# Moving transposes, projections and channel-major steps later in the slots of an attention loop

## The chip, the cores and the metric

The kernel runs on one core of one Trainium2 chip. The metric is the device time of one execution in microseconds; the median of three runs of the kernel before is 972.73 us (972.63 to 973.1). Five engines work in parallel, each through its own instructions in a fixed order: TensorE (PE; its weight loads are listed as PEld), VectorE (DVE), ScalarE (ACT), GpSimd (POOL) and SyncE (SP), which issues the DMA transfers.

## The reference

Four residual layers over 512 frames of 1024 channels: a pooling mixer, a gated MLP with a causal convolution, chunked attention with 16 heads of 64 channels, and a second gated MLP. The change touches the attention alone. What it computes:

```python
h = rmsnorm(x, mix_norm[i])
qkv = h @ w_qkv
q = head_rmsnorm(q, q_norm)          # per head, over its 64 channels
k = head_rmsnorm(k, k_norm)
s = einsum('bqhd,bkhd->bhqk', qc, kb) * scale + bias   # band of 9 chunks of 64 keys
p = softmax(where(valid, s, -1e30))
o = einsum('bhqk,bkhd->bqhd', p, vb)
x = x + o @ w_o
```

All values are float32. The kernel makes its products from a high and a low part of each factor, with three matmuls for one product in the projections.

## The kernel before

The attention is the middle of the program. Queries and keys are projected in four groups, `project(0)` to `project(3)`; group c holds heads 4c to 4c + 3, so it feeds head pairs 2c and 2c + 1. Each projection accumulates four tiles in PSUM over 96 matmuls (L123 to L125, tiles `qk`). The tiles are then copied out as `Z[c, t]` (L964 on DVE, L966 on ACT), squared (L956), reduced (L957) and normalised: a chain of small steps (L974, L975, L135 and L136 on ACT, L137 to L139, L977) makes one factor per frame and head, and L979 multiplies the four `Z` tiles by it on POOL.

Per head pair two channel-major steps (`channel_major`, four transposes each at L1032, tiles `zt`) turn the normalised queries and then the keys. Four DMA moves on SP (L1046) put halves where the second head of the pair needs them.

The 16 heads make 64 tiles of 128 queries, one tile a slot of the loop. In its slot i a tile goes through these steps, in this order on PE:

- `scores` of tile i: two matmuls (L1062, L1063), then on DVE the bias and row minimum (L1066), on ACT the exponential and its sum (L1068), on DVE a reciprocal (L1069), on ACT the scaling (L1070, tile `sb`);
- a channel-major step of the next pair, where i modulo 8 is in `CM`;
- `turn` of tile i - LAG: one to four transposes (L1078, tiles `tp`), which ACT and DVE split into high and low parts (L102, L103, tiles `pt`);
- after the last tile of a head, LAGM slots later, `mix`: eight matmuls with the values (L1090, tiles `oo`), copied by ACT (L1095) and added by DVE into the pair's output (L1096).

All PSUM tiles of these steps, `sc`, `zt`, `tp` and `oo`, share four banks (tag "S"). Each `sb` tile of a place in a head has one buffer.

Between the steps PE runs matmuls of a filler: `project(1)` up to slot FE[0], `project(2)` up to FE[1], `project(3)` up to FE[2], and from there the output projection of the first six pairs (L123 to L125, tiles `wo`, added to `X` at L1016) up to slot 64 + FO. `fill(upto)` issues as many of its matmuls as are due at that point of a slot. A pair's output is split into high and low parts (L102, L103, tiles `two`) before the output projection reads it.

PE's order in the loop is thus written by hand with the numbers LAG, LAGM, FE, FO and CM. The orders of DVE, ACT, POOL and SP are made by the framework's scheduler at build time.

Of the kernel before, what the change touches and what calls it, by code (L numbers as in the profile page):

```python
# [43 lines left out]
BANKS = {"PQ": 2, "SS": 4}  # L44


LAG, LAGM = 2, 2
FE = (3.5, 19.5, 35.5)
FO = LAG + 6
CM = (2, 3)  # L50


KIND = "uuppp" + "s" * 17
# [19 lines left out]
def trunk(ctx: ExitStack, tc: tile.TileContext, xt, xT, cols, band, edge, poolw, gv, wout, wqk, wv, wo, rel, out):  # L73
# [23 lines left out]
    def split(raw, hi, lo, eng=None, eng_hi=None):  # L97

        if eng_hi:
            eng_hi.tensor_copy(hi, raw)  # L100
        else:
            nc.scalar.activation(hi, raw, AF.Copy)  # L102
        return (eng or nc.vector).tensor_sub(lo, raw, hi.bitcast(F32))  # L103
# [23 lines left out]
    def run(steps):  # L127
        step = None
        for step in steps:
            pass  # L130
        return step
# [785 lines left out]
    def attention():  # L917
# [104 lines left out]
        def outputs():  # L1022
            yield from output(range(4))
            yield from output((4, 5))

        def channel_major(p, i):


            zt = psum("S", f"zt{p}_{i}", 4)
            for t in range(TT):  # L1030
                j = 4 * i + 2 * (p % 2)
                nc.tensor.transpose(zt[:, t * P:(t + 1) * P], Z[p // 2, t][:, j:j + 2, :].rearrange("p h d -> p (h d)"), ident)  # L1032
            zh, z2 = (big.tile([P, S], F32R, name=f"z{c}{p}_{i}", tag="zqk", bufs=8) for c in "h2")
            zl = None if i else g_tile(f"zl{p}_{i}")
            if i:
                nc.scalar.activation(zh, zt, AF.Copy, scale=gq[:, i:i + 1])
                for e in range(2):
                    hs = slice(e * HD, (e + 1) * HD)
                    nc.vector.scalar_tensor_tensor(KL[p % 2][e][hs], zt[hs], gq[hs, i:i + 1], zh[hs].bitcast(F32), op0=OP.mult, op1=OP.subtract)
            else:  # L1040
                split_scaled(zt, gq[:, i:i + 1], zh, zl)

            nc.gpsimd.tensor_copy(z2[HD:], zh[HD:].bitcast(F32))
            moves = [(z2[:HD], (z2 if i else zl)[HD:]), (zh[HD:], (zh if i else zl)[:HD])]
            for o, x in moves:
                nc.sync.dma_start(o.bitcast(F32), x if x.dtype == F32 else x.bitcast(F32))  # L1046
            QK[p, i] = (zh, z2)

        def scores(h, t):

            p, e = divmod(h, 2)
            q, k, kl = QK[p, 0][e], QK[p, 1][e], KL[p % 2][e]
            if t == 0:

                base = rdram[h, :]
                for r, n in ((0, S - HD), (HD, S)):
                    nc.sync.dma_start(BT[h % 2][r:r + HD, S - n:], bass.AP(tensor=base.tensor, offset=base.offset + HD, ap=[[1, HD], [1, n]]))
            n = (t + 1) * P
            nw = max(n, 256)

            sc = psum("S", f"sc{h}_{t}", 4)
            nc.tensor.matmul(sc[:, :nw], q[:, t * P:n], k[:, :nw], start=True, stop=False)  # L1062
            nc.tensor.matmul(sc[:, :nw], q[:, t * P:n], kl[:, :nw], start=False, stop=True)  # L1063
            SM[h, t] = s_ = big.tile([P, n], F32, name=f"sb{h}_{t}", tag=f"sb{t}")
            mx = tmp.tile([P, 3], F32, name=f"mx{h}_{t}", tag="mx", bufs=4)
            nc.vector.tensor_tensor_reduce(out=s_[:, :n], in0=sc[:, :n], in1=BT[h % 2][:, :n][:, ::-1], scale=1.0,  # L1066
                                           scalar=3e38, op0=OP.add, op1=OP.min, accum_out=mx[:, 0:1])
            nc.scalar.activation(s_[:, :n], s_[:, :n], AF.Exp, scale=-1.0, bias=mx[:, 0:1], accum_out=mx[:, 1:2])  # L1068
            nc.vector.reciprocal(mx[:, 2:3], mx[:, 1:2])  # L1069
            nc.scalar.activation(s_[:, :n], s_[:, :n], AF.Copy, scale=mx[:, 2:3])  # L1070

        def turn(h, t):

            n = (t + 1) * P
            s_ = SM.pop((h, t))
            tp = psum("S", f"tp{h}_{t}", 4)
            for j in range(t + 1):
                nc.tensor.transpose(tp[:, j * P:(j + 1) * P], s_[:, j * P:(j + 1) * P], ident)  # L1078
            split(tp[:, :n].rearrange("p (j q) -> p j q", q=P), *(x[:, t:4 * t + 1:3] for x in PT[h % 2]))

        def mix(h):

            p, e = divmod(h, 2)
            hs = slice(e * HD, (e + 1) * HD)
            oo = psum("S", f"oo{h}", 4)
            if p not in O2:
                O2[p] = big.tile([P, S], F32, name=f"o2_{p}", tag="o2", bufs=4)
            for c in range(2):
                for j in range(TT):
                    nc.tensor.matmul(oo[:, j * P:], V[j, h // 4][:, h % 4].rearrange("p a d -> p (a d)"),  # L1090
                                     PT[e][c][:, 4 * j:3 * j + TT].rearrange("p t q -> p (t q)"),
                                     start=j == 0 and c == 0, stop=j == TT - 1 and c == 1)
            ob = g_tile(f"ob{h}")
            other = slice(HD - e * HD, 2 * HD - e * HD)
            nc.scalar.activation(ob[hs], oo[other], AF.Copy)  # L1095
            nc.vector.tensor_add(O2[p][hs], oo[hs], ob[hs])  # L1096
# [13 lines left out]
        nb = len(tiles_)  # L1110
        fillers = [(project(1), 96, -3, FE[0]), (project(2), 96, FE[0], FE[1]), (project(3), 96, FE[1], FE[2]), (outputs(), 144, FE[2], nb + FO)]

        with tc.manual_schedule(engines={mybir.EngineType.PE}):
            cur, done, kept = 0, 0, 0

            def fill(upto):

                nonlocal cur, done
                while cur < len(fillers):
                    g, n, a, b = fillers[cur]  # L1120
                    due = n * (upto - a) / (b - a)
                    while done < min(due, n):
                        next(g)
                        done += 1
                    if upto < b:
                        return
                    run(g)
                    cur, done = cur + 1, 0

            fill(0)  # L1130
            for i in range(nb + LAG + LAGM):
                steps = []
                if i < nb:
                    steps.append(lambda: scores(*tiles_[i]))
                if i % 8 in CM and i // 8 + 1 < NPAIR:
                    steps.append(lambda: channel_major(i // 8 + 1, CM.index(i % 8)))
                j = i - LAG
                if 0 <= j < nb:
                    steps.append(lambda: turn(*tiles_[j]))
                j2 = j - LAGM  # L1140
                if 0 <= j2 < nb and j2 % TT == TT - 1:
                    steps.append(lambda: mix(tiles_[j2][0]))
                for x, step in enumerate(steps):
                    step()
                    if late and x < 2:
                        late.pop(0)()
                    fill(i + (x + 1) / len(steps))

                while 8 * kept + 7 <= j2 and (cur == 3 or cur == 2 and done >= 24 * (kept // 2 + 1)):
                    split(O2[kept], XS[kept], XS[KD + kept])  # L1150
                    kept += 1
            fill(nb + FO)
# [37 lines left out]
    with tc.tile_pool(name="ba", bufs=1) as big:  # L1190
        rest = attention()
# [55 lines left out]
```

## Time and profile before

| | before |
|---|---|
| median of three runs | 972.73 us |
| profiled execution, its own time | 972.73 us |
| its span, first to last instruction | 970.9 us |
| PE busy in the span | 962.8 us |
| attention loop, 456.4 to 606.2 us | 149.8 us |
| PE busy in it | 147.86 us |
| ACT busy in it | 131.23 us |
| DVE busy in it | 115.44 us |
| POOL busy in it | 62.46 us |

A row of the timeline gives start and length in us, engine, line, operation, written tile <- read tiles, shape and how many such instructions it merges; in brackets the idle time of the engine ahead of it and what ended it. A row of waits gives engine, line and tile, what it waited for, the sum in us, how often, and the longest. A row of the chain of waits gives start, length, engine and line. A row of DMA issues ends with the median us from issue to landing. Records of matmuls overlap, so a busy PE is not necessarily at its peak.

### The profile page before, as it was taken

What the parts mean: (1) busy time and instruction counts of PE and PEld (TensorE: products, weight loads), DVE (VectorE), ACT (ScalarE), POOL (GpSimd) and SP (SyncE); (2) the same over time, 40 slices, a digit from 0 to 9 for tenths busy, and PEclk for the clock granted to TensorE, in tenths of its full rate; (3) what the DMA queues carried; (4) which work ended last, traced back from release to release, by engine and by line L of the source; (5) the groups of instructions that cost most, each with busy time, mean ns of one, the idle gap of its engine ahead of it and who ended that gap; (6) DMA issues with size and microseconds to landing.
All of it is one profiled execution on the core that took longest, in us unless ns stands there. A gap on an engine that the chain in (4) does not pass through costs nothing.

```text
span 970.9 us, 13813 instructions
## 1 busy us (share of the span) xinstructions
PE 962.8 (99%) x5038; PEld 819.1 (84%) x5038; DVE 804.9 (83%) x1452; ACT 575.4 (59%) x990; POOL 103.1 (11%) x90
## 2 busy tenths in 40 slices
PE   9999999999999999999999999999999999999998
PEld 8788988888888888888888787888998888888886
DVE  8999989999899855442777888999989999989953
ACT  7665554655555544345898988646555565566531
POOL 2300000000000013204534532000000000000000
PEclk9999999999999999999999999999999999999999
DMA  8222332332323234332343341332323233332323
GB/s 342 73 96 71 114 107 81 120 119 88 108 77 119 78 84 147 92 121 92 111 115 106 97 118 55 101 108 80 116 91 102 89 120 106 107 101 79 114 81 110
DMA packets 37428, 102.83 MB, mean 106 GB/s; under 512 B 4432, under 2 KB 7904, under 8 KB 37360
## 3 DMA queue, kind: packets, MB, share of 16 engines
q1 hardware_dynamic: 37296, 101.90, 32.4%
q8 instruction: 40, 0.66, 0.3%
q14 instruction: 28, 0.23, 0.1%
q0 software_dynamic: 32, 0.04, 0.0%
q10 hardware_dynamic: 32, 0.00, 0.0%
HBM read 95.60 MB, written 2.14 MB: 101 GB/s over the span
## 4 chain that ended last, share of the span: by engine, by line
PE 94%; DVE 4%; ACT 2%; issue 0%; DMA 0%; DVEq 0%; ACTq 0%
PE st_m L610 11%; PE out L124 8%; PE out L125 8%; PE out L123 8%; PE st_m L612 5%; PE st_t L610 5%; PE gv L124 4%; PE gv L125 4%; PE gv L123 4%; PE qk L124 3%; PE qk L123 3%; PE qk L125 3%; PE st_t L612 3%; PE st_b L610 3%; PE tp L1078 2%; PE oo L1090 2%
## 5 line engine op out<-in xcount | busy, mean ns | idle before, releaser
L124 PE MATMUL out<-one,ow_h 128*128 128x512 f32 x224 | 88.0, 393 | 0.0
L123 PE MATMUL out<-one,ow_h 128*128 128x512 f32 x224 | 87.8, 392 | 0.0
L125 PE MATMUL out<-one,ow_l 128*128 128x512 f32 x224 | 87.8, 392 | 0.0
L833 DVE TENSOR_TENSOR X<-out,X 128x512 f32<-128x512 f32 (+1 forms) x65 | 44.3, 682 | 50.2 <-PE out L125 49.9
L409 ACT ACTIVATE ow_h<-wo_r 128x640 fp32r<-128x640 f32 (+1 forms) x64 | 50.4, 787 | 55.0 <-PE out L124 46.5
L610 PE MATMUL st_m<-two,g_h 128*128 128x512 f32 x224 | 70.0, 394 | 0.0
L610 PE MATMUL st_m<-h,g_h 128*128 128x512 f32 x224 | 69.1, 389 | 0.0
L410 DVE TENSOR_TENSOR ow_l<-wo_r,ow_h 128x640 fp32r<-128x640 f32 (+1 forms) x64 | 56.8, 888 | 2.5 <-ACT ow_h L409 2.5
L424 DVE SCALAR_TENSOR_TENSOR c<-a,col,c 128x511 f32<-128x511 f32 (+1 forms) x76 | 56.6, 747 | 0.0
L125 PE MATMUL qk<-wqk_h,two 128*128 128x512 f32 x128 | 51.4, 402 | 0.0
L123 PE MATMUL qk<-wqk_h,two 128*128 128x512 f32 x128 | 50.8, 409 | 0.0
L124 PE MATMUL qk<-wqk_l,two 128*128 128x512 f32 x128 | 50.8, 397 | 0.0
L610 PEld LDWEIGHTS st_m<-h,g_h 128*128 128x128 f32 x224 | 42.1, 188 | 9.6
L619 ACT ACTIVATE w<-st_m 128x512 f32<-128x512 f32 x28 | 16.7, 598 | 56.0 <-PE st_m L612 56.0
L612 PEld LDWEIGHTS st_m<-two,g_l 128*128 128x128 f32 x224 | 42.0, 188 | 8.8
L610 PEld LDWEIGHTS st_m<-two,g_h 128*128 128x128 f32 x224 | 41.1, 188 | 9.3 <-ACT w L619 0.8
L124 PEld LDWEIGHTS out<-one,ow_h 128*128 128x128 f32 x224 | 42.3, 189 | 6.3 <-DVE one L435 0.3
L125 PEld LDWEIGHTS out<-one,ow_l 128*128 128x128 f32 x224 | 42.3, 189 | 6.3
L123 PEld LDWEIGHTS out<-one,ow_h 128*128 128x128 f32 x224 | 42.3, 189 | 6.0
L1066 DVE CUSTOM_DVE_ANT_0 sb<-sc,B 128x128 f32<-128x128 f32 (+1 forms) x64 | 31.1, 486 | 18.9 <-PE sc L1063 18.0
L612 PE MATMUL st_m<-h,g_l 128*128 128x256 f32 x224 | 45.1, 283 | 0.0
L421 ACT ACTIVATE c<-a,col 128x512 f32<-128x512 f32 x38 | 30.7, 813 | 23.8 <-DVE a L768 22.0
(378 smaller groups left out, 2999.5 us busy)
## 6 DMA issues: line engine op xcount, KB each, us to landing
gv_r<-gv SPq DMA_DIRECT2D x86, 512.0 KB, 3.8
wo_r<-wout SPq DMA_DIRECT2D x32, 384.0 KB, 3.1
wo_r<-wout SPq DMA_DIRECT2D x32, 320.0 KB, 2.9
wqk_r<-wqk SPq DMA_DIRECT2D x16, 512.0 KB, 3.4
wv_r<-wv SPq DMA_DIRECT2D x8, 512.0 KB, 3.5
wo_r<-wo SPq DMA_DIRECT2D x8, 512.0 KB, 3.4
xt<-xt SPq DMA_DIRECT2D x4, 512.0 KB, 5.3
X<-xT SPq DMA_DIRECT2D x8, 256.0 KB, 7.3
```

The costliest lines, as they stand in the source:

```text
L123: yield nc.tensor.matmul(o, sh, mh, start=first, stop=False, **how)
L124: yield nc.tensor.matmul(o, sh, ml, start=False, stop=False, **how)
L125: yield nc.tensor.matmul(o, sl, mh, start=False, stop=last, **how)
L409: nc.scalar.activation(hi[:, :n], raw[:, :n], AF.Copy)
L410: return hi, lo, lambda: nc.vector.tensor_sub(lo[:, :n], raw[:, :n], hi[:, :n].bitcast(F32))
L421: nc.scalar.activation(c, a, AF.Identity, scale=cw[2], bias=cw[3])
L424: nc.vector.scalar_tensor_tensor(c[:, j:], a[:, :S - j], cw[2 - j], c[:, j:], op0=OP.mult, op1=OP.add)
L610: nc.tensor.matmul(o, hi[:, c], B[i, name], start=first and i == 0, stop=False, **how)
L612: nc.tensor.matmul(o[:, 0], lo[:, c], B[i, name][:, 0], start=False, stop=i == 3, **how)
L833: nc.vector.tensor_add(X[d][:, fs], o[:, fs], X[d][:, fs])
L1066: nc.vector.tensor_tensor_reduce(out=s_[:, :n], in0=sc[:, :n], in1=BT[h % 2][:, :n][:, ::-1], scale=1.0, scalar=3e38, op0=OP.add, op1=OP.m ...
L1078: nc.tensor.transpose(tp[:, j * P:(j + 1) * P], s_[:, j * P:(j + 1) * P], ident)
```

## The change

```diff
-LAG, LAGM = 2, 2
-FE = (3.5, 19.5, 35.5)
+LAG, LAGM = 3, 2
+FE = (5.5, 21.5, 37.5)
 FO = LAG + 6
-CM = (2, 3)
+CM = (3, 4)
...
                     fill(i + (x + 1) / len(steps))
+                fill(i + 1)
```

A tile's transposes now come three slots behind its scores, and with them the mix of a head, five slots behind its last scores instead of four. The three later projections end at slots 5.5, 21.5 and 37.5, and the channel-major steps stand in slots 3 and 4 of each eight. FO follows LAG, so the spread of the output projection ends at slot 73 instead of 72. The new `fill(i + 1)` acts only in a slot without steps, of which there is one near the end.

The same instructions are issued on every engine; their order changes. Three places follow. In the names, a number behind `sc`, `sb`, `mx` or `tp` is the head and the tile (`sc10_2`: head 10, third tile), behind `zt` the pair and query or key step, behind `qk` or `z` the projection, behind `o2` the pair, and the last number is only a buffer's.

DVE, the last steps of the normalisation of `project(3)`, which feeds pairs 6 and 7. Before:

```order
L137 SCALAR_TENSOR_TENSOR qk3_t_4894<-qk3_y_4893 128x32
L1066 ISA sb9_3_5496,mx9_3_5497<-sc9_3_5493,B1_3660 128x512
L1066 ISA mx9_3_5497 128x1
L1069 RECIPROCAL mx9_2_5478<-mx9_2_5478 128x1
L138 TENSOR_TENSOR qk3_t_4894<-qk3_t_4894,qk3_a_4892 128x32
L139 SCALAR_TENSOR_TENSOR qk3_y_4893<-qk3_t_4894,qk3_y_4893 128x32
L977 TENSOR_TENSOR qk3_y_4893<-qk3_y_4893,n1_y_3806 128x32
```

Now:

```order
L1096 TENSOR_TENSOR o2_4_5518<-oo8_5517,ob8_5527 64x512
L137 SCALAR_TENSOR_TENSOR qk3_t_4935<-qk3_y_4934 128x32
L138 TENSOR_TENSOR qk3_t_4935<-qk3_t_4935,qk3_a_4933 128x32
L1066 ISA sb10_2_5554,mx10_2_5555<-sc10_2_5551,B0_3659 128x384
L1066 ISA mx10_2_5555 128x1
L139 SCALAR_TENSOR_TENSOR qk3_y_4934<-qk3_t_4935,qk3_y_4934 128x32
L1069 RECIPROCAL mx10_1_5536<-mx10_1_5536 128x1
L977 TENSOR_TENSOR qk3_y_4934<-qk3_y_4934,n1_y_3806 128x32
```

L977, the last step ahead of POOL's L979, stood behind the L1066 of head 9, tile 3, and stands behind that of head 10, tile 2.

PE, from the scores of head 10, tile 2 to the first channel-major step of pair 6. Now:

```order
L1063 MATMUL sc10_2_5551<-kl10_3653,zh5_0_5341 128x384
L124 MATMUL wo1_0_5515<-two5_101,wo0_0_h_5439 128x512
L125 MATMUL wo1_0_5515<-two1_97,wo0_0_l_5440 128x512
L1078 MATMUL tp9_3_5562<-ident_106,sb9_3_5483 128x128 x4
L123 MATMUL wo1_0_5515<-two1_97,wo0_0_h_5439 128x512
L124 MATMUL wo1_0_5515<-two5_101,wo0_0_h_5439 128x512
L1062 MATMUL sc10_3_5571<-zh5_1_5379,zh5_0_5341 128x512
L1063 MATMUL sc10_3_5571<-kl10_3653,zh5_0_5341 128x512
L125 MATMUL wo1_0_5515<-two1_97,wo0_0_l_5440 128x512
L1032 MATMUL zt6_0_5581<-ident_106,z3_0_5316 128x128
```

Before, the channel-major step stood ahead of the scores of head 10, tile 3, one slot earlier; the transposes of head 9, tile 3 stood ahead of the scores of tile 2 and come after them now.

DVE, the same steps of the normalisation of `project(2)`, which feeds pairs 4 and 5. Before:

```order
L138 TENSOR_TENSOR qk2_t_4399<-qk2_t_4399,qk2_a_4397 128x32
L1069 RECIPROCAL mx5_2_4980<-mx5_2_4980 128x1
L139 SCALAR_TENSOR_TENSOR qk2_y_4398<-qk2_t_4399,qk2_y_4398 128x32
L1066 ISA sb5_3_4998,mx5_3_4999<-sc5_3_4995,B1_3660 128x512
L1066 ISA mx5_3_4999 128x1
L103 TENSOR_TENSOR pt1l_3650<-tp5_0_4988,pt1h_3649 128x128
L977 TENSOR_TENSOR qk2_y_4398<-qk2_y_4398,n1_y_3806 128x32
L103 TENSOR_TENSOR two4_100<-o2_1_4749,two0_96 128x512
```

Now:

```order
L1066 ISA sb6_1_5036,mx6_1_5037<-sc6_1_5033,B0_3659 128x256
L1066 ISA mx6_1_5037 128x1
L138 TENSOR_TENSOR qk2_t_4430<-qk2_t_4430,qk2_a_4428 128x32
L139 SCALAR_TENSOR_TENSOR qk2_y_4429<-qk2_t_4430,qk2_y_4429 128x32
L1096 TENSOR_TENSOR o2_2_5020<-oo4_5019,ob4_5029 64x512
L977 TENSOR_TENSOR qk2_y_4429<-qk2_y_4429,n1_y_3806 128x32
L103 TENSOR_TENSOR two4_100<-o2_1_4748,two0_96 128x512
```

L977 moved behind L1066 of head 6, tile 1 and behind L1096, the addition of the mix of head 4; the split of pair 1's output (`two4`) still follows it.

## The prediction

> **What bounds the kernel now.** I read the page's busy times first, then busy time in windows over the attention loop, the waits there, and the timeline at the places that stood out.
>
> ```profile
> span 970.9 us, 13813 instructions
> PE 962.8 (99%) x5038; PEld 819.1 (84%) x5038; DVE 804.9 (83%) x1452; ACT 575.4 (59%) x990; POOL 103.1 (11%) x90
> ```
>
> TensorE (PE) sets the end. Its instructions are the same in both kernels, in another order, so only its waits can move the time. The changed numbers act in the attention loop, 456 to 606 us. Columns: window, length, busy time of PE, weight loads, VectorE (DVE), ScalarE (ACT), GpSimd (POOL), granted clock, DMA.
>
> ```profile
> 540.00:560.00 20.00, 19.09 (x108) 15.23 (x107) 17.23 (x55) 18.05 (x48) 9.84 (x10) 1.00 0.27 78
> ...
> 600.00:610.00 10.00, 9.19 (x48) 7.40 (x47) 7.79 (x15) 6.36 (x12) 0.00 (x0) 1.00 0.17 54
> ```
>
> PE is idle 0.91 us in the first and 0.81 in the last of these windows. That undercounts, as the next rows show: a matmul is recorded for 0.39 us, but the next starts 0.23 us after it, so 0.16 us of each wait lies under a record. I price waits by starts.
>
> ```profile
> 589.57 0.39 PE L125 MATMUL wo<-two,wo_l 128*128 128x512 f32 x1
> 589.80 0.40 PE L123 MATMUL wo<-two,wo_h 128*128 128x512 f32 x1
> 590.37 0.33 PE L1078 MATMUL tp<-ident,sb 128*128 128x128 f32 x1 [0.18 <-ACT sb L1070]
> ...
> 599.96 0.75 PE L1090 MATMUL oo<-pt0h,one 128*128 128x512 f32 x4
> 600.55 0.80 PE L1090 MATMUL oo<-pt0l,one 128*128 128x512 f32 x4
> 601.18 0.44 PE L124 MATMUL wo<-two,wo_h 128*128 128x512 f32 x1
> 601.91 0.55 PE L1078 MATMUL tp<-ident,sb 128*128 128x128 f32 x3 [0.28 <-ACT sb L1070]
> ...
> 604.58 0.78 PE L1090 MATMUL oo<-pt1h,one 128*128 128x512 f32 x4
> 605.88 0.50 PE L1090 MATMUL oo<-pt1l,one 128*128 128x512 f32 x1 [0.53 <-DVE pt1l L103]
> ```
>
> Transposes (L1078) wait for ACT's scaled scores (L1070), and the last mix (L1090) for DVE's low parts (L103): 0.57 - 0.23 = 0.34, 0.73 - 0.23 = 0.50 and 1.30 - 0.59 = 0.71 us (0.59 is the same step unhindered, 599.96 to 600.55). Two more:
>
> ```profile
> 549.85 0.50 PE L124 MATMUL wo<-two,wo_h 128*128 128x512 f32 x1 [0.67 <-DVE two L103]
> ...
> 551.68 0.40 PE L123 MATMUL wo<-two,wo_h 128*128 128x512 f32 x1
> 552.17 0.44 PE L1078 MATMUL tp<-ident,sb 128*128 128x128 f32 x2
> ```
>
> The output projection waits for the split of a finished head pair, 0.67 shown and 0.16 hidden, 0.8 us, and a transpose 0.49 - 0.23 = 0.26. Last, a place that waits for nothing yet, the channel-major transposes of pair 6 (L1032), which read what POOL normalises at L979:
>
> ```profile
> 552.80 0.19 DVE L139 SCALAR_TENSOR_TENSOR qk_y<-qk_t,qk_y 128x32 f32<-128x32 f32 x1
> 553.03 0.19 DVE L977 TENSOR_TENSOR qk_y<-qk_y,n_y 128x32 f32<-128x32 f32 x1
> 553.30 4.05 POOL L979 TENSOR_TENSOR z<-z,qk_y 128x512 f32<-128x512 f32 x4 [5.82 <-DVE qk_y L977]
> 557.49 0.34 PE L1063 MATMUL sc<-kl,zh 128*128 128x384 f32 x1
> 557.86 0.56 DVE L1066 CUSTOM_DVE_ANT_0 sb<-sc,B 128x384 f32<-128x384 f32 x1
> 557.89 0.60 PE L1032 MATMUL zt<-ident,z 128*128 128x128 f32 x4
> 558.34 0.08 DVE L1066 DVE_READ_ACCUMULATOR2_ANT mx<- 128x1 f32 x1
> ```
>
> POOL ends at 557.35 and PE starts at 557.89: 0.54 us to spare. For pair 4 the same spare is 520.70 - 518.59 = 2.11 us:
>
> ```profile
> 514.09 4.50 POOL L979 TENSOR_TENSOR z<-z,qk_y 128x512 f32<-128x512 f32 x4 [5.55 <-DVE qk_y L977]
> 520.70 0.44 PE zt L1032 x4
> ```
>
> **The change part by part.** FE puts the end of each later projection two slots later, CM the channel-major step that reads its result one slot later. From the one to the other stay 11 - 5.5 = 5.5 slots of 10 - 3.5 = 6.5. A slot is (557.89 - 520.70) / 16 = 2.3 us, from the first channel-major step of pair 4 to that of pair 6, so every spare shrinks by about that. Pair 6 has none left.
>
> *Pair 6.* The order makes it sharper. DVE's L977 now stands behind the softmax step L1066 of head 10, tile 2, and that waits for PE's scores sc10_2; before, it stood behind head 9, tile 3, three score steps earlier. Count from T, the start of the second sc10_2 matmul (L1063). L1066 starts at T + 0.37 (557.49 to 557.86), the next instruction 0.48 later, L977 another 0.23 (552.80 to 553.03), POOL 0.27 after that, and its four products take 4.05: T + 5.40. On PE follow 0.18 for the scores, two matmuls, four transposes, two matmuls, the two 512-wide scores and a matmul. From these rows and the first fence on PE:
>
> ```profile
> 588.31 0.60 PE L1078 MATMUL tp<-ident,sb 128*128 128x128 f32 x4
> 588.66 0.48 PE L123 MATMUL wo<-two,wo_h 128*128 128x512 f32 x1
> 588.98 0.40 PE L124 MATMUL wo<-two,wo_h 128*128 128x512 f32 x1
> 589.39 0.34 PE L1063 MATMUL sc<-kl,zh 128*128 128x384 f32 x1
> ```
>
> four transposes cost 0.35 and 0.09 more on the matmul behind them (588.66 to 588.98 is 0.32, not 0.23), so 0.18 + 0.46 + 0.44 + 0.46 + 0.46 + 0.23 = 2.23, and the fourth channel-major transpose is due 0.3 later, at T + 2.5. PE waits 5.4 - 2.5 = **2.9 us**. Bounds 2.4 (all handovers at 0.1) and 3.3 (POOL at 4.50). Both sides hang on the same T, so earlier waits cancel.
>
> *Pairs 2 and 4.* L977 now stands behind the head addition L1096, which waits for the mix. T is the start of the second sc6_1 matmul; the mix's second half starts 0.63 (600.55 to 601.18) and two short steps before it, about 1.0.
>
> ```profile
> 593.16 0.80 PE L1090 MATMUL oo<-pt1l,one 128*128 128x512 f32 x4
> ...
> 594.94 0.69 DVE L1096 TENSOR_TENSOR o<-oo,ob 64x512 f32<-64x512 f32 x1
> ```
>
> L1096 comes 1.78 after that half, so at T + 0.8; DVE reaches it at about T + 1.05, after L1066 (0.37, and under 0.48 for its two parts), L138 and L139. L977 is 0.6 later, POOL 0.27 later: T + 5.95 with products of 4.05, T + 6.4 with 4.50. PE gets to the fourth transpose after 14 matmuls (3.22), seven transposes (0.61, and 0.18 behind them), the rest of three score steps (0.12, half a 512-wide matmul, then 0.36 and 0.46) and 0.3: T + 5.25. So 0.7 us for pair 2 and, where DVE's next row is the same split of a head pair as at 514.13, 1.15 for pair 4: **1.85**, bounds 0 and 2.4.
>
> ```profile
> 514.13 1.55 DVE L103 TENSOR_TENSOR two<-o,two 128x512 fp32r<-128x512 f32 x1
> ```
>
> That split took 1.55 us there beside POOL's 4.50. [...]
>
> *The later transposes* take away the waits for scaled scores and, with two more fills ahead of it, the last mix's: 0.34 + 0.50 + 0.26 + 0.71 = **-1.8 us** (bounds -2.2 with smaller ones, -1.2 if one stays).
>
> *The split's wait* of 0.8: the split of pair 3 is put out at the end of slot 36 for the tenth output matmul, due at 37.5 + 9 / 4.06 = 39.7; before, at the end of slot 35 for 35.5 + 9 / 3.95 = 37.8. So it has 2.7 slots instead of 1.8, but waits behind the same queue on ACT and DVE. I take half, **-0.4** (0 to -1.1).
>
> *Closer spacing in the channel-major slots.* PE now goes from one step to the next past 256-wide scores instead of 512-wide ones (two matmuls of 0.23), and DVE has the longest L1066 just ahead. The banks of the score ring come free up to 0.35 us later against PE, in six such pairs: 0 to 2.1; today only pairs 6 and 7 show such waits, so I take a quarter, **+0.5**. The rest (fills per slot 96 / 8.5 = 11.3 instead of 96 / 6.5 = 14.8 at first, and 144 / 35.5 = 4.06 for 144 / 36.5 = 3.95 at the end) moves no work off PE.
>
> Sum: 2.9 + 1.85 - 1.8 - 0.4 + 0.5 = +3.05. The profiled execution took 972.73 us, its span of 970.9 and 1.83 around it, and is itself the median of the three runs: 972.73 + 3.05 = **975.8 us**.
>
> **Rivals.**
> 1. *More is taken away than starts show (the other side).* The waits of PE's weight loads (PEld) count in full, since the loads end last in these steps.
>
> ```profile
> PEld tp L1078 <- ACT sb L1070: 3.1, 8, 0.6
> PEld wo L124 <- DVE two L103: 1.0, 1, 1.0
> PEld oo L1090 <- DVE pt1l L103: 0.7, 1, 0.7
> ```
>
> Then 4.8 go instead of 2.2: 2.9 + 1.85 + 0.5 - 4.8 = +0.45, 973.2 us, not slower by what can be told. It decides from 3.3 of these 4.8 on. Against it: loads run ahead of matmuls, and where starts can be compared they lost 0.26 to 0.50 on a transpose, with 0.6 the longest wait of a load. Chance 0.07.
> 2. *Pairs 2 and 4 keep their cover.* The spare of 2.11 nearly outlasts the slot; only pair 6 waits, and no bank does: 972.73 + 2.9 - 1.8 - 0.4 = 973.4. For it: spare and slot are within 0.2. Against it: L1096 ahead of L977. Chance 0.19.
> 3. *Pair 6's halves land late.* They are moved by DMA before the scores of pair 6 read them.
>
> ```profile
> 563.65 0.54 SPq L1046 DMA_DIRECT2D zh<-zh  x1
> zh<-zh SPq DMA_DIRECT2D x8, 128.0 KB, 2.3
> 574.13 0.44 PE zt L1032 x4
> ```
>
> The first transposes at 557.89 led to the last move at 563.65 and a landing 2.3 later, 8.1 us. From there to the first score five slots stay of six, each (574.13 - 557.89) / 8 = 2.0 now: 10.1, less the part of the slot ahead of the transposes. If over 1 us of the remainder goes, pairs 6 and 7 add 1 each: 977.8. Chance 0.08.
>
> 4. *The gap slows the clock.* Every window above has a granted clock of 1.00, with gaps up to 0.8 us. If a gap of 2.9 let it fall to half for as long, it would cost 1.4 more: 977.2. [...] Chance 0.03.
>
> **How the numbers follow.** The forecast has 0.63, with a range of its own of 974.5 to 977.2. 8 in 10 with the rivals: 973.4 (rival 2) to 977.8 (rival 3). A measurement here tells 0.2% (1.95 us) from no change. Slower by more, above 974.7: 0.63 + 0.08 + 0.03, less 0.02 for the forecast's low end, 0.72. Faster, under 970.8: only rivals 1 and 2 together get there (2.9 - 4.8 = -1.9), 0.03. Within: the rest, 0.25.
>
> **What would show it.** Right: PE's transposes L1032 of pair 6 wait for POOL's L979 in three steps of about 0.8, 2.5 to 3.3 us together; those of pairs 2 and 4 by 0.4 to 1.3 each; no wait of L1078 for L1070 and none at the last mix. Wrong: pair 6's transposes start with no wait, or L977 runs before sc10_2; a wait of scores (L1062) for a DMA (rival 3); a clock under 1.00 after 560 us (rival 4).

## The result, and the profile after

The changed kernel takes 977.51 us (median of four executions: 976.59, 977.45, 977.57, 977.98), the kernel before 972.71 beside it: a ratio of 1.0047, 95% interval 1.0035 to 1.0060. It is slower by 4.8 us. The forecast was 975.8, its range 973.4 to 977.8. The profiled execution took 977.57. Three of the four had a mean granted clock of 0.998; the one of 976.59 had 1.0. The page and the waits of PE in the attention loop:

```profile
span 975.8 us, 13790 instructions
PE 964.4 (99%) x5038; PEld 820.6 (84%) x5038; DVE 805.4 (83%) x1452; ACT 574.3 (59%) x990; POOL 102.5 (11%) x90
```

```profile
PE zt L1032 <- POOL z L979: 3.3, 5, 0.7
PE wo L124 <- DVE two L103: 0.9, 1, 0.9
PE oo L1090 <- DVE zl L108: 0.4, 1, 0.4
PE tp L1078 <- ACT ob L1095: 0.3, 1, 0.3
PE sc L1062 <- DMA zh<-zh: 0.2, 1, 0.2
```

PE is *busy* 1.6 us longer with the same 5038 instructions. That is no wait; it fits the fall of the clock, below. The waits for scaled scores and at the last mix are gone, and the channel-major transposes now wait for POOL's L979, at pairs 2, 4 and 6. The timeline of PE there, and POOL's products for pairs 4 and 6:

```profile
480.71 0.49 PE L1032 MATMUL zt<-ident,z 128*128 128x128 f32 x3
481.80 0.33 PE L1032 MATMUL zt<-ident,z 128*128 128x128 f32 x1 [0.60 <-POOL z L979]
...
520.67 0.80 PE L1032 MATMUL zt<-ident,z 128*128 128x128 f32 x3
522.14 0.33 PE L1032 MATMUL zt<-ident,z 128*128 128x128 f32 x1 [0.67 <-POOL z L979]
...
557.12 0.35 PE L1063 MATMUL sc<-kl,zh 128*128 128x384 f32 x1
559.13 0.40 PE L125 MATMUL wo<-two,wo_l 128*128 128x512 f32 x1
559.57 0.33 PE L1032 MATMUL zt<-ident,z 128*128 128x128 f32 x1
560.58 0.33 PE L1032 MATMUL zt<-ident,z 128*128 128x128 f32 x1 [0.68 <-POOL z L979]
561.58 0.33 PE L1032 MATMUL zt<-ident,z 128*128 128x128 f32 x1 [0.67 <-POOL z L979]
562.58 0.33 PE L1032 MATMUL zt<-ident,z 128*128 128x128 f32 x1 [0.67 <-POOL z L979]
562.66 0.48 PE L123 MATMUL wo<-two,wo_h 128*128 128x512 f32 x1
```

```profile
517.65 4.44 POOL L979 TENSOR_TENSOR z<-z,qk_y 128x512 f32<-128x512 f32 x4 [6.27 <-DVE qk_y L977]
...
558.48 4.04 POOL L979 TENSOR_TENSOR z<-z,qk_y 128x512 f32<-128x512 f32 x4 [7.44 <-DVE qk_y L977]
```

Counted by starts against an unhindered group, pair 2 loses 0.79 us, pair 4 1.17, and pair 6 2.92 (0.21 ahead of its first transpose, 2.71 behind it). The windows behind that gap (the column before the last two is the granted clock):

```profile
562.00:563.00 1.00, 0.42 (x3) 0.39 (x4) 0.00 (x0) 0.11 (x2) 1.00 (x2) 1.00 0.43 130
563.00:564.00 1.00, 1.00 (x6) 0.81 (x5) 0.34 (x1) 0.80 (x2) 0.75 (x2) 0.72 0.00 0
564.00:565.00 1.00, 1.00 (x6) 0.82 (x5) 0.82 (x4) 0.00 (x0) 0.36 (x1) 0.50 0.00 0
565.00:566.00 1.00, 1.00 (x6) 0.82 (x5) 0.00 (x0) 0.37 (x1) 0.00 (x0) 0.50 0.41 94
566.00:567.00 1.00, 1.00 (x5) 0.86 (x4) 0.65 (x1) 0.97 (x4) 0.61 (x1) 0.57 0.73 168
567.00:568.00 1.00, 1.00 (x9) 0.96 (x7) 0.95 (x3) 0.00 (x0) 0.93 (x1) 1.00 0.00 0
```

The granted clock is halved from about 563.44 to 566.86 us. What it lost is 0.28 + 0.50 + 0.50 + 0.43 = 1.71 us of full speed. Three smaller places complete the account:

```profile
551.03 0.48 PE L123 MATMUL wo<-two,wo_h 128*128 128x512 f32 x1
552.38 0.50 PE L124 MATMUL wo<-two,wo_h 128*128 128x512 f32 x1 [0.88 <-DVE two L103]
...
582.05 0.48 PE L124 MATMUL wo<-two,wo_h 128*128 128x512 f32 x1
582.93 0.79 PE L1090 MATMUL oo<-pt1h,one 128*128 128x512 f32 x3 [0.40 <-DVE zl L108]
...
589.26 0.39 PE L123 MATMUL wo<-two,wo_h 128*128 128x512 f32 x1
589.88 0.36 PE L1062 MATMUL sc<-zh,zh 128*128 128x256 f32 x1 [0.24 <-DMA zh<-zh]
```

Where nothing hinders it, a matmul starts 0.23 us after one of 512 columns, 0.18 after one of 384, and 0.31 to 0.32 after one that follows transposes. So the split of pair 3 costs 1.35 - 0.32 = 1.03 us (1.01 before, in two places), PSUM banks 0.88 - 0.31 = 0.57 here and 0.45 at 506.6 us (five such places, 0.95 us in all, before), and the first scores of pair 7 wait for a DMA, 0.39. Pair 6's scores wait for none.

### The profile page after: what moved, and what is told of

It reads as the page before. It is cut to its first block, busy times and chain, and to the rows that moved or that the text cites. A ratio compares the mean times of both kernels' runs of the same rounds, so it can differ in the third digit from the quotient of the medians.

```text
span 975.8 us, 13790 instructions
## 1 busy us (share of the span) xinstructions
PE 964.4 (99%) x5038; PEld 820.6 (84%) x5038; DVE 805.4 (83%) x1452; ACT 574.3 (59%) x990; POOL 102.5 (11%) x90
## 5 line engine op out<-in xcount | busy, mean ns | idle before, releaser
L612 PE MATMUL st_m<-two,g_l 128*128 128x256 f32 x224 | 44.4, 280 | 0.0
```

What stands on the lines that cost most here:

```text
L612: nc.tensor.matmul(o[:, 0], lo[:, c], B[i, name][:, 0], start=False, stop=i == 3, **how)
```

## The experiments

The kernels differ from the changed one by the lines shown; times are medians beside runs of the kernel before on the same chip (972.8 to 973.0). A measure without the scatter of the program's start and end is the stretch from the first channel-major transposes (L1032) to the statistics of the norm that follows the attention (L154). In the kernel before it is 222.99 us:

```profile
409.31 0.38 PE L1032 MATMUL zt<-ident,z 128*128 128x128 f32 x2
...
632.30 0.95 PE L154 MATMUL f_st<-ones,f_sq 128*128 128x1 f32 x8
```

In the changed one it lasts from 409.16 to 637.21 us, 228.05 us.

**Parts of the change.**

```diff
-FE = (5.5, 21.5, 37.5)
+FE = (3.5, 19.5, 35.5)
-CM = (3, 4)
+CM = (2, 3)
```

> Only the third slot of lag is kept (LAG 3); the projections' ends (FE 3.5, 19.5, 35.5) and the channel-major places (CM 2, 3) are those of before. Theory A (the loss sits in the waits of the z transposes on GpSimd's L979, which the later ends of the projections brought, and in the clock behind pair 6): no zt wait on POOL over 0.3 us, no clock below 0.95 between 556 and 570 us, the five waits of the score transposes (2.0 us) gone, the waits for the split (two) and for PSUM banks 1 to 2.5 us longer than before; estimate from the trace's durations in the new order 0.7 us over before: 973.4 us (972.5 to 974.3). Rival B (the third slot itself is what costs, by banks of PSUM that come free later): 976 us or more.

975.88 us, 1.0032 (1.0019 to 1.0044), the stretch 225.89. It lies between the two theories: no zt wait and no fall of the clock, as A has it, but 2.5 us more than its estimate. The waits of PE:

```profile
PE oo L1090 <- DVE kl L1039: 2.1, 3, 0.8
PE wo L123 <- ACT two L102: 1.7, 1, 1.7
PE tp L1078 <- DVE pt0l L103: 0.9, 1, 0.9
```

The first is the one that rival B named, banks. The ring has four: with LAG 3 the mix moves from the slot of the keys' channel-major step to the next one, and the fourth tile after that step's `zt` is then the mix's `oo`, which waits for the DVE step that still reads `zt` (L1039). The second is the split, one slot later for the same end of the projection. The third stands behind a long split on DVE, which comes back below.

```diff
-LAG, LAGM = 3, 2
+LAG, LAGM = 2, 2
```

> Only the later places are kept (FE 5.5, 21.5, 37.5 and CM 3, 4); the transposes come two slots behind their scores, as before. Theory A (the third slot takes out waits of the score transposes that would otherwise be there, and later places bring the zt waits): zt waits of pair 6 about 2 to 3 us, and waits of tp L1078 on ACT or DVE of about 1 us each at the second tile of several heads between 455 and 640 us, 5 us or more in all; estimate 7.8 us over before: 980.5 us (978.5 to 982). Rival B (the third slot costs): less than after's 977.5 us. Rival C (the two parts are independent, the third slot worth the 2.0 us of waits that went): 979.5 us, with tp waits of about 2.0 us.

986.93 us, 1.0144 (1.0130 to 1.0158), above all three.

```profile
PE tp L1078 <- ACT sb L1070: 6.9, 6, 2.1
PE sc L1062 <- DVE pt0l L103: 2.5, 1, 2.5
PE zt L1032 <- POOL z L979: 1.3, 2, 0.7
```

So the third slot does not cost with these ends, it saves: theory A's 5 us or more of transposes are there. The 2.5 us of `sc` on DVE and the clock (0.995 to 0.997 over every execution) it did not have. They come back below.

```diff
-FE = (5.5, 21.5, 37.5)
+FE = (4.5, 20.5, 36.5)
```

> After with the projections' ends one slot earlier (FE 4.5, 20.5, 36.5 for 5.5, 21.5, 37.5), LAG 3 and CM 3, 4 kept. Theory A (pair 2, 4 and 6 wait only because the z transposes stand before the end of GpSimd's four products L979): zt waits on POOL fall from 4.7 us in all to under 1.0, no clock below 0.95 behind pair 6, tp waits stay under 0.6; estimate from the trace's durations 1.6 us under before: 971.1 us (970 to 972.3), the fastest so far. Rival B (the lag's third slot and the channel-major places cost about as much as they bring): 973 to 975 us.

973.78 us, 1.0011 (1.0002 to 1.0020), but eleven executions from 971.74 to 976.42, where the kernel before has 972.5 to 973.5. In the profiled one (973.37) the zt waits on POOL are gone, the stretch takes 221.98 us, 1.0 under before, and 0.9 was lost ahead of it and 0.8 behind it, where the two programs are the same. The mechanism is theory A's, the time rival B's.

Next, the lag and the channel-major places of the change with the ends of before:

```diff
-FE = (5.5, 21.5, 37.5)
+FE = (3.5, 19.5, 35.5)
```

> The third slot of lag and the later channel-major places (LAG 3, CM 3, 4) with the projections' ends of before (FE 3.5, 19.5, 35.5). The lag alone took 975.9 us, 3.1 more than before, with waits of oo and tp for PSUM banks (2.1 and 0.9 us) and of the split (1.7 us). Theory A (the lag must go with projections and channel-major steps that are later too: with early ends the split of pair 3 and the banks come late): waits of about 1.6 us at wo for the split and of 1 to 3 us at oo and tp for banks stay, zt waits none; estimate from the trace's durations 1.4 us over before, with the same miss as for the lag alone 976 us (974.2 to 977.2). Rival B (the channel-major places alone were wrong for the lag, one slot later mends it): no bank waits over 0.3 us, 973 us or less.

977.28 us, 1.0044 (1.0031 to 1.0057): just over theory A's range, with a fall of the clock in three of five executions (976.3 and 976.5 without). The wait for the split is 2.0 us, that of `oo` for banks 0.2. So CM one slot later does mend the bank waits of the lag, and early ends leave the split late. Then the ends one slot later with the channel-major places of before:

```diff
-FE = (5.5, 21.5, 37.5)
+FE = (4.5, 20.5, 36.5)
-CM = (3, 4)
+CM = (2, 3)
```

> LAG 3 with the projections' ends one slot later than before (FE 4.5, 20.5, 36.5) and the channel-major places of before (CM 2, 3). Theory A (the z transposes wait where their place comes ahead of the end of L979; ends and places moved apart by one slot bring a part of the wait of after back): a zt wait of pair 6 of about 1 us, not 2.9, clock 1.00; estimate from the trace's durations 1.5 us under before, and 0.2 over the same with CM 3, 4, so 973 to 975 us by what that kernel took. Rival B (with CM 2, 3 the banks are late as with the lag alone): bank waits at oo and tp of 2 us or more, 975.5 us or more.

975.31 us, 1.0027 (1.0018 to 1.0037), between the two ranges. The zt wait is 0.7 and a bank wait of `oo` 0.5, as theory A has it. New is a wait of 1.8 us, `tp` on DVE, at 587 us. The next kernel has the same.

```diff
-FE = (5.5, 21.5, 37.5)
+FE = (4, 20.5, 36.5)
```

> As the kernel with ends one slot later (FE 4.5, 20.5, 36.5, CM 3, 4, LAG 3), but its first end half a slot earlier (FE 4, 20.5, 36.5). Theory A (between the two ends, at which the split and the banks or the z transposes are late, lies a flat stretch a little under before): no zt wait over 0.3 us, bank waits about 1.5 us in all, estimate from the trace's durations 1.7 us under before, 972 us (971 to 973.5), and as little jitter as before, should the scatter of the kernel with 4.5 (971.7 to 976.4 us) come from its chance state of transfers at the start and end. Rival B (the scatter belongs to the new order): runs 2 us or more apart again.

975.92 us, 1.0033 (1.0020 to 1.0046): theory A missed, by 2.4 us over its range, and rival B's sign came, with executions from 975.05 to 978.09, 3.0 us apart. Its wait, and the rows of DVE and POOL that make it:

```profile
PE tp L1078 <- DVE mx L1066: 1.8, 1, 1.8
```

```profile
584.26 2.38 POOL L103 TENSOR_TENSOR wo_l<-wo_r,wo_h 128x1024 fp32r<-128x1024 f32 x1
584.49 2.70 DVE L103 TENSOR_TENSOR two<-o,two 128x512 fp32r<-128x512 f32 x1
587.11 0.68 DVE L1066 CUSTOM_DVE_ANT_0 sb<-sc,B 128x512 f32<-128x512 f32 x1
```

**One instruction of DVE behind one of POOL.** The split of a pair takes DVE 0.68 us elsewhere. Here it ends 0.55 us after POOL's subtraction, which started first. In the kernel with ends at 4.5 the two start within 0.02 us, and POOL's is the long one:

```profile
584.17 2.98 POOL L103 TENSOR_TENSOR wo_l<-wo_r,wo_h 128x1024 fp32r<-128x1024 f32 x1
584.19 0.68 DVE L103 TENSOR_TENSOR two<-o,two 128x512 fp32r<-128x512 f32 x1
```

Which of these two was issued first can't be told from 0.02 us. In the kernel before DVE's starts first, and again POOL's is the long one:

```profile
582.32 0.68 DVE L103 TENSOR_TENSOR two<-o,two 128x512 fp32r<-128x512 f32 x1
582.35 2.92 POOL L103 TENSOR_TENSOR wo_l<-wo_r,wo_h 128x1024 fp32r<-128x1024 f32 x1
```

The same ending, 0.54 or 0.55 us behind POOL's, shows in two more kernels: lag alone (the split from 586.11 us for 2.25, POOL's subtraction from 585.41 for 2.41) and no lag (549.36 for 2.44, 548.88 for 2.37). It is the 2.5 us of the kernel without lag and the wait of `tp` for `pt0l` of the lag alone. The change has one too, at 530.43 us (2.15 us, 0.80 behind the start of a POOL subtraction of 2.40), where PE waits for nothing, and the split of 1.55 us at 514.13 before ends 0.55 us behind the first of POOL's four products (1.04 us from 514.09). Where the rows tell an order, the one that started second is the long one, in both orders: DVE's took 2.15 to 2.70 us for 0.68 where POOL's had started 0.23 to 0.80 us before it, and POOL's 2.92 for the 2.41 that it took at 561.98 in the same kernel, where DVE's had started 0.03 us before it. That the second stands until the first has ended is the author's reading of them. The test takes the length of POOL's instruction away and leaves PE's order as it is:

```diff
-        return (eng or nc.vector).tensor_sub(lo, raw, hi.bitcast(F32))
+        return nc.vector.tensor_sub(lo, raw, hi.bitcast(F32)) if not eng else [
+            eng.tensor_sub(lo[:, i:i + 256], raw[:, i:i + 256], hi[:, i:i + 256].bitcast(F32))
+            for i in range(0, 1024, 256)]
```

On the kernel with ends at 4, 20.5, 36.5:

> The kernel with ends at 4, 20.5, 36.5 (975.9 us), whose 2.0 us wait at 586 us stands behind one split of VectorE, two L103, that took 2.70 us for 0.68 while GpSimd's wo_l L103 (2.38 us) ran, started 0.23 us before it. Changed: GpSimd makes each L103 in four quarters of 256 columns, about 0.6 us each; TensorE's order is the same. Theory A (VectorE's split stood until GpSimd's one instruction ended): VectorE can get in between quarters, the split there takes 1.4 us or less, the wait of tp L1078 falls from 1.8 us to 0.6 or less, and the time to 974.3 us (973.3 to 975), with fewer executions at a clock of 0.998. Rival B (the two share throughput, whatever the size): the split stays over 2 us and the time within 0.5 us of 975.9.

975.09 us for 975.92, a little over the range. The wait of `tp` on L1066 falls from 1.8 to 0.2, the stretch from 226.57 to 224.31 us (the first of these held a fall of the clock, below, the second none), and the split to

```profile
585.34 3.28 POOL L103 TENSOR_TENSOR wo_l<-wo_r,wo_h 128x256 fp32r<-128x256 f32 x4
585.63 0.99 DVE L103 TENSOR_TENSOR two<-o,two 128x512 fp32r<-128x512 f32 x1
```

Theory A holds: the split ends at 586.62, again about 0.55 us behind POOL, but behind the end of its first quarter (about 586.08: 585.34 and the 0.73 to 0.75 us of single quarters at 563.00 and 550.34). What it stood behind is one instruction of POOL: beside the whole subtraction it took 2.70 us, beside the quarters 0.99, where a share of throughput, as rival B has it, would have left it over 2 us. Other waits, 0.7 us for a bank and 0.7 for a DMA, took a part of the gain. On the kernel with ends at 4.5, 20.5, 36.5:

> The kernel with ends one slot later (4.5, 20.5, 36.5; 973.8 us, executions from 971.7 to 976.4), with GpSimd's L103 in four quarters. In its profile VectorE's split at 584.19 us and GpSimd's wo_l at 584.17 us start within 0.02 us of each other; the split took 0.68 and GpSimd 2.98 us. Theory A (who comes first there differs between executions, and costs 2 us, more with the clock's fall, when it is GpSimd): the executions lie within 1.5 us, the highest under 973.5, the median 971.8 us (970.9 to 972.6), under before's. Rival B (the scatter comes from transfers at the start and end of the program, which took 0.9 and 0.8 us more than before's in that execution): a scatter of 2 us or more stays, median 973 to 974.

973.00 us, 0.9999 (0.9991 to 1.0008). The scatter goes as theory A has it, from 4.7 to 0.84 us (972.61 to 973.45); the two were run on different chips, but on both the kernel before scatters by 1.0 us. The gain that theory A promised does not come: the stretch took 222.68 us, 0.3 under before. What took it up is not shown; POOL's four quarters took 3.27 us there for the 2.98 of the whole. And on the kernel before:

> The kernel before with GpSimd's L103 in four quarters and nothing else, as the measure of what the quarters bring by themselves; orders of TensorE, VectorE and ScalarE are the same. In before's profile the one split that was long was that at 514.13 us (1.55 us), and those at 582.32 us came 0.03 us ahead of GpSimd's. Theory A (before has no long split on the path that sets its end): 972.6 us (972.2 to 973.1). Rival B (quarters help every kernel alike): 971 us or less. Rival C (four starts for one cost GpSimd time that is on the path): 973.5 us or more.

972.98 us, 1.0000 (0.9991 to 1.0009): theory A. No version here beats the kernel before by what can be told.

**The wait on POOL and the clock.**

```diff
-                    nc.gpsimd.tensor_mul(Z[c, t], ...)
+                    (nc.vector if c and t > 1 else nc.gpsimd).tensor_mul(Z[c, t], ...)
```

> After with two of the four products L979 of each later group (t = 2 and 3) on VectorE in place of GpSimd, so that GpSimd's chain of 4.0 us falls to about 2.1 us; nothing else is changed. Theory A (the z transposes of pairs 2, 4 and 6 wait for the end of that chain, and pair 6's gap of 3 us is what brings the clock down): the waits of zt L1032 on z fall from 3.3 us to about 1.0, no clock below 0.95 between 560 and 570 us; estimate from the trace's durations 0.4 us under before, so with VectorE's extra 2 us in pair 6 about 973.0 us (972 to 974.3). Rival B (the transposes are held by something behind the products, or VectorE's queue then is what is late): 976 us or more, with waits of zt or of the score transposes on VectorE of 2 us or more.

974.50 us, 1.0016 (1.0007 to 1.0025), 3.0 less than the change, just over theory A's range. The zt waits fall to 1.5 us for the 1.0 expected, by starts 0.59 at pair 4 and 1.9 at pair 6 (0.2 of it ahead of the first transpose), and all eleven executions keep a clock of 0.999 or more. So POOL's four products are what the transposes wait for, and the fall of the clock goes with the gap. To part the clock from the gap, matmuls fill it:

```diff
             zt = psum("S", f"zt{p}_{i}", 4)
+            if p == 6 and i == 0:
+                for _ in range(11):
+                    nc.tensor.matmul(zt, QK[5, 0][0][:, :P], QK[5, 1][0], start=True, stop=True)
```

> After with eleven matmuls of 512 columns added ahead of pair 6's z transposes, 2.5 us at the pitch of 0.23 us; what they write is overwritten, so that they only keep TensorE busy while GpSimd makes its products. Theory A (the three gaps of 0.67 us there made the clock fall to 0.50 to 0.72 for some 4 us afterwards, which costs about 1.0 to 1.5 us): the four transposes end where they did or up to 0.3 us later, granted clock 1.00 from 563 to 570 us, 976.2 us (975.9 to 976.6, runs close together). Rival B (the clock falls for another reason, load for instance): the clock falls all the same and the time is 977.5 us or up to 0.3 us more.

975.78 us, 1.0034 (1.0021 to 1.0047), 1.73 less than the change, with more work on PE. The last transpose starts 0.2 us later, at 562.78, and the clock stays:

```profile
559.55 2.66 PE L1032 MATMUL zt<-zh,zh 128*128 128x512 f32 x11
562.78 0.33 PE L1035 MATMUL zt<-ident,z 128*128 128x128 f32 x1 [0.23 <-POOL z L979]
```

```profile
563.00:564.00 1.00, 1.00 (x8) 0.82 (x7) 0.13 (x1) 0.85 (x2) 0.76 (x2) 1.00 0.02 8
564.00:565.00 1.00, 1.00 (x9) 0.85 (x8) 1.00 (x4) 0.09 (x1) 0.57 (x1) 1.00 0.00 0
```

So the fall goes with the gap: it came in three of the change's four executions and in none of these five. Its size, 1.7 us of the change's 4.8, is the 1.71 of the windows. The times agree, with 1.73, but only roughly: the change's one execution without a fall took 976.59, 0.98 less than the median of the other three, and these five lie between 975.67 and 976.97. By the profiles the stretch falls from 228.05 to 226.04 us, 2.0, with 0.39 of it for the DMA wait, which is not there either. How much filling it takes:

```diff
-                for _ in range(11):
+                for _ in range(5):
```

> After with five matmuls of 512 columns in place of eleven ahead of pair 6's z transposes: 1.15 us of the 2.9 us are filled, and about 1.7 us of gap are left in pieces. In the kernels so far the longest stretch of waiting was 1.7 and 1.9 us where no execution had a clock of 0.998 or less, 2.0 and 2.3 us where about half had, and 2.6 and 2.9 us where 3 of 4 or all had. Theory A (it goes by the length of the gap, with a step near 2 us): clock 0.999 or 1.0 in all executions, 976.0 us, as with eleven (975.8). Rival B (only a TensorE that is kept busy throughout holds the clock): some executions at 0.998, 977 us or more.

976.05 us, all six executions at a clock of 1.0. Theory A holds: with 1.7 us of gap left, in pieces, the clock stayed. Over all kernels, the longest gap by starts in the profiled execution, and how many executions had a mean clock of 0.998 or less:

| kernel | gap, us | fallen |
|---|---|---|
| before | 1.0, in pieces | 0 of 28 |
| gap filled by eleven, by five | 1.2 (pair 4), 1.7 | 0 of 5, 0 of 6 |
| the three with quarters | up to 1.0 | 0 of 33 |
| ends 4.5, 20.5, 36.5 | 1.0 | 2 of 11 |
| half on VectorE | 1.9 | 0 of 11 |
| lag alone | 1.85 | 0 of 6 |
| ends 4.5, CM 2, 3; ends 4 | 2.00, 2.00 | 4 of 10, 2 of 5 |
| ends of before, CM 3, 4 | 2.17 | 3 of 5 |
| no lag | 2.64 | 4 of 4 |
| the change | 2.92, in pieces | 3 of 4 |

Near 2 us it fell in some executions and not in others of the same kernel (9 of 20 at 2.00 to 2.17 us, 7 of 8 at 2.64 and 2.92); how long the gap was in those without a profile is not known. The two with ends at 4.5 (976.4 us) fit if GpSimd came first in them; no profile of these two shows it. The kernel with ends at 4 fell in its profile, about 2.8 us after PE stopped (586.12 to 588.96):

```profile
586.00:587.00 1.00, 0.12 (x1) 0.00 (x0) 1.00 (x1) 0.00 (x0) 0.64 (x1) 1.00 0.00 0
587.00:588.00 1.00, 0.06 (x1) 0.09 (x2) 1.00 (x4) 0.17 (x1) 0.00 (x0) 1.00 0.00 0
588.00:589.00 1.00, 1.00 (x5) 0.71 (x6) 0.99 (x7) 1.00 (x4) 0.00 (x0) 0.98 0.02 8
589.00:590.00 1.00, 1.00 (x6) 0.90 (x5) 0.54 (x2) 1.00 (x4) 0.00 (x0) 0.50 0.45 124
...
592.00:593.00 1.00, 1.00 (x7) 0.75 (x6) 0.79 (x3) 0.69 (x3) 0.00 (x0) 0.81 0.33 131
```

From 588.96 to 592.38 is 3.42 us, as from 563.44 to 566.86 in the change; the kernel without lag fell for 6.8 us, twice that.

## Why the prediction was right or wrong

The side and the range were right: slower, 977.51 within 973.4 to 977.8. The forecast's own figure was 1.7 us short, as much as the clock took, and that the rest comes out in sum is partly luck: the split and the DMA cost 0.4 us each that the forecast did not have, the banks 0.4 and the later transposes 0.2 less than it had. The range held the result with the help of rival 3, for whose DMA its upper end was set; one execution, 977.98, lies above it. The terms against the account by starts of the profiled execution:

| term | predicted | measured |
|---|---|---|
| pair 6 behind POOL's L979 | +2.9 | +2.92 |
| pairs 2 and 4 | +0.7, +1.15 | +0.79, +1.17 |
| later transposes and the last mix | -1.8 | -2.0 (with two smaller waits) |
| the split of pair 3 | -0.4 | 0.0 |
| banks of the ring | +0.5 | +0.1 |
| DMA ahead of pair 7's scores | a rival | +0.4 |
| clock | a rival | +1.7 |
| sum | +3.05 | +5.1 |

The sum agrees with the stretch, 228.05 - 222.99 = 5.06 us. The start of the program was 0.15 us shorter in this execution, and the medians differ by 4.8.

- *Pair 6* went by the steps of the prediction: POOL's end was put at T + 5.40, and 557.12 + 5.40 is 562.52, where 558.48 + 4.04 is. The kernel with half of the products on VectorE confirms the cause.
- *Pairs 2 and 4* came as priced: POOL's products took 4.05 us for pair 2 and 4.44 for pair 4, against 4.05 and 4.50. Only the split of pair 1 beside them took 0.68 us and not 1.55: it started 0.15 us ahead of POOL, at 517.50, and not 0.04 behind it.
- *The later transposes* did take the waits away. Without the third slot such waits come to 6.9 us, and the kernel is 9.4 us slower still.
- *The split's wait* was mis-sized. The prediction gave it 2.7 slots for 1.8 and took half a gain. The mix that it waits for moves a slot with the lag, and DVE's instructions ahead of it with it: 1.03 us for 1.01.
- *The banks* cost 0.1 more, against +0.5. The price came from the right ring and the wrong pair: it is the mix behind the keys' step that counts, and CM moved with the lag keeps these two in one slot. Where only the lag moved, they cost 2.1 us.
- *Rival 3*, the DMA, showed in a small form, 0.39 us at pair 7 and none at pair 6; the remainder of slots was nearly enough.
- *Rival 4*, the clock, is what happened, with 977.2 predicted for it and a chance of 0.03. That chance was the author's estimate; no gap in the loop of before is over 1.0 us. A half clock stands in the trace of before behind the program's last matmul, 0.50 from 969.56 us to the end at 970.9, where PE had stopped at 966.97; in the change PE stopped as long at the end, from 971.89 to 975.8, and the clock stayed at 1.00. Three transposes in the gap did not keep the clock: PE was busy for a third of each microsecond there (0.33, 0.33 and 0.42), and the clock fell to 0.50, for 3.42 us and not for the 2.9 of the estimate. The 3.4 us ahead of the falls in the change and in the kernel with ends at 4 held 1.5 and 1.6 us of PE's records, and the longest stretches of the loop without one are 0.88 and 1.83 us, so neither fall had a stop of PE of 2 us ahead of it. Why a kernel with a gap of 2.0 us fell in 4 of 10 executions, and why two falls lasted 3.42 us and one 6.8, no run here shows.
- *Rivals 1 and 2* are out: what starts show is what went, and pairs 2 and 4 lost their cover.

## What to carry to other kernels

Numbers that set an order belong together: one slot more of lag wanted the channel-major steps and the projections' ends one slot later as well, and with the ends two slots later the consumer came ahead of a 4 us chain on GpSimd. Price a gap on TensorE with a possible fall of the clock behind it, even when short instructions break it up: here a gap of 2.92 us brought 1.7 us more, in three of four executions, and gaps of 2.00 to 2.64 us a fall in 13 of 24. Where subtractions of VectorE and GpSimd like these splits come at about the same time, ask who starts first: 0.23 us decided over 2 us (2.70 for 0.68), and with GpSimd's in quarters the scatter of one kernel fell from 4.7 to 0.84 us.

## What the runs showed of the hardware that was not expected

In three profiles the clock fell to 0.50 behind gaps of 2.00 to 2.92 us on TensorE, for 3.42 us in two of them (the change, ends at 4) and 6.8 us in the third (no lag); a mean clock of 0.998 or less, as these three have, came in 16 of 28 executions of the five kernels with such gaps. A subtraction of VectorE of 0.68 us took 2.15 to 2.70 us when a subtraction of GpSimd of 2.4 us had started 0.23 to 0.80 us before it, and that of GpSimd took 2.92 us when VectorE's had started 0.03 us before it, and 2.98 when the two starts were 0.02 us apart. What stays open is the start of the program, where nothing was changed: TensorE reached its first channel-major transposes between 409.16 and 410.23 us over the profiled executions, a scatter of 1.1 us, and what follows the stretch took 0.8 us longer in two of them than in the others. No run here was made to find the cause.
